# Unused words in the pools, so that tiles read by one-pass matmuls start on multiples of 128 bytes

## The chip, the cores and the metric

The kernel runs on one core of one Trainium2 chip. The metric is the device time of that core in microseconds (us), the median of several runs. The profile comes from one profiled execution; its engines are PE (TensorE matmuls), PEld (TensorE weight loads), DVE (VectorE), ACT (ScalarE), POOL (GpSimd) and SP (the engine that issues most DMAs).

## The reference, cut to what matters

Two layers over a stream of 256 context tokens and 2048 latent tokens, 1024 wide, all in float32. Each layer does, on every token:

```
h      = layer_norm(x) * (1 + scale) + shift           # modulated by c or c_ctx
z      = h @ w_in                                      # 1024 x 3040 columns
y      = concat(hgrn2(z), latent_attention(z), gla(z)) * silu gates
x_new  = layer_norm(ALPHA * x + gate * (y @ w_out)) * ln_g + ln_b
```

The recurrences run in both directions; the attention has 4 heads over all tokens with 128-wide compressed keys and a 64-wide rotary part. The result is the latent stream after layer 1.

## The kernel before, in words

Each layer has three stages, one behind the other, each in a context with its own pools. `project` makes the normed tokens and multiplies them with w_in. `mix` runs attention and recurrences side by side. `output` multiplies by w_out and does the post norm.

**One-pass matmuls.** A float32 operand a is split by `split` into a part hi in the format F32R and a rest lo, also in F32R. The product a b is then three matmuls, hi hi + hi lo + lo hi, each of them one pass through the array. A matmul has a stationary operand (128 columns, loaded by a weight load of its own) and a moving one (256 or 512 columns, streamed past). These are the one-pass matmuls of the kernel, with the pools' tiles that they read:

- L417 in `group`, natural order: stationary hh or hl (the split tokens), moving wh or wl (the split weights), 256 columns (224 in the first weight group), 48 in a row for one pair of token tiles.
- L428 in `group`, transposed order: stationary wh or wl, moving hh or hl, 256 columns, 48 in a row.
- L838 and L850 in `query_group`: mh, ml, urh, url against cqh, cql, 256 columns, 6 in a row for one output tile.
- L888 to L892 in `attend`: stationary qh, ql, rh, rl, moving cth, ctl, ks, up to 512 columns, 5 in a row.
- L913, L914 and L917 in `attend`: stationary cnh, cnl, moving ph, pl, 256 columns.
- L1069 to L1071 in `output`: stationary yhl, moving the 16 weight tiles wh[k], wl[k] (name wo), 512 columns, 24 in a row for one output tile. The first 11 weight tiles lie under tag woa, the last five (wl[5], wh[6], wl[6], wh[7], wl[7]) under tag wob.
- L564: two small ones for the forget gates, with zaT and wa2.

In these rows of a profile the moving operand stands first behind the arrow and the stationary one second (`pj<-wh,hh`). Transposes and the recurrences' matmuls (L774, L790, L801, L623) take plain float32 tiles.

**Where tiles lie.** A pool's tiles are laid in memory one behind the other, by tag in the order of first use, each rounded up to a multiple of 32 bytes for each partition. Pools follow each other in the order in which they are made, and `Route` only names which tags share a pool. So the start of a tile follows from the sizes in front of it. The first tile, ident, starts on a multiple of 128 bytes. In front of mh stand 512 + 32 + 32 + 384 + 4 x 64 + 2 x 64 + 1024 + 32 = 2400 bytes, which is 18 x 128 + 96, so mh starts 96 bytes behind a multiple of 128. What follows in cpool is a multiple of 128, so every stage's first pool starts at 96 as well. In `project` two small pools shift what comes behind them: the side work of layer 0 (bmc, mp, bmd, gcol) adds 288 bytes to multiples of 128, the statistics (st, mv, ve, rs) another 288. In layer 1 a tile `pad` of 16384 bytes stands in place of the side work. In `output` the statistics (sto, mvo, veo, rso) add 288.

The offsets of the operands behind a multiple of 128 bytes, before and after the change, worked out in this way:

| tile | before, layer 0 | before, layer 1 | after, both |
|---|---|---|---|
| hh, hl | 96 | 96 | 0 |
| wh, wl in `project` | 32 | 0 | 0 |
| mh, ml, urh, url, cqh, cql, qh, ql, rh, rl, cth, ctl, ks, cnh, cnl, ph, pl | 96 | 96 | 0 |
| wo under woa | 96 | 96 | 0 |
| wo under wob, yhl | 0 | 0 | 0 |
| wa2, zaT | 64 | 64 | 96 |

A slice of such a tile starts a multiple of 512 bytes behind its start, so the offsets hold for every matmul. The order of instructions on each engine comes from a scheduler that works with priorities and modelled times; a tile that takes the memory of earlier tiles waits until their last readers are done.

Of the kernel before, what the change touches and what calls it, by code (L numbers as in the profile page):

```python
# [31 lines left out]
def view(ap, offset, dims, parts=None):  # L32
    """A free-dimension pattern of its own on the tile behind ap."""
    pd = list(ap.ap[0])
    if parts is not None:
        pd[1] = parts
    return bass.AP(ap.tensor, ap.offset + offset, [pd] + [list(d) for d in dims])


class Route:  # L40
    """Tiles by tag, each from the pool that holds the tag: the order of pools is the order in memory."""
# [12 lines left out]
class Trunk:  # L54
# [17 lines left out]

    def split(self, hi, lo, src, hi_eng="act", lo_eng="dve"):
        """src = hi + lo with both parts in the tensor engine's one-pass format."""
        nc = self.nc
        if hi_eng == "act":
            nc.scalar.copy(hi, src)  # L77
        else:
            nc.vector.tensor_copy(hi, src)
        if lo_eng == "pool":  # L80
            nc.gpsimd.tensor_tensor(lo, src, hi, op=ALU.subtract)
        else:
            nc.vector.tensor_tensor(lo, src, hi, op=ALU.subtract)  # L83

    def rsqrt(self, pool, v, n, name):
        """(v + eps already added) ** -0.5 for a [P, n] tile."""
        r = pool.tile([P, n], F32, tag=name, name=name)
        self.nc.gpsimd.tensor_tensor(r, v, self.mhalf[:, :n], op=ALU.pow)
        return r

    def constants(self):
        nc, io, c = self.nc, self.io, self.cpool
        self.ident = c.tile([P, P], F32, name="ident")
        make_identity(nc, self.ident)
        self.mhalf = c.tile([P, 8], F32, name="mhalf")
        nc.vector.memset(self.mhalf, -0.5)
        # the gated heads' query scale, on the rows of the even and of the odd heads
        self.hm = c.tile([P, 2], F32, name="hm")
        for r in range(4):
            for i in range(2):  # L100
                nc.vector.memset(self.hm[32 * r:32 * r + 32, i:i + 1], float(32.0 ** -0.5) if r % 2 == i else 0.0)
        self.mask = c.tile([P, 6, 64], U8, name="mask")
        with self.tc.tile_pool(name="cm", bufs=1) as cm:
            mf = cm.tile([P, 6, 64], F32, name="mf")
            nc.sync.dma_start(out=mf, in_=io["lmask"])
            nc.vector.tensor_copy(self.mask, mf)

# [1 line left out]
    def scratch(self, l):  # L109
        """Layer l's arrays in DRAM, and its modulation columns."""  # L110
        d, c, nt = self.dpool, self.cpool, self.nt
        S = {}
        S["scT"] = c.tile([P, KD, 2], F32, name=f"scT{l}")
        S["shT"] = c.tile([P, KD, 2], F32, name=f"shT{l}")
        S["gate"] = d.tile([2, D], F32, name=f"gate{l}")
        S["F"] = d.tile([P, self.ntiles, 2, 3, SEG], F32, name=f"dF{l}")
        S["K"] = d.tile([P, self.ntiles, 2, 3, SEG], F32, name=f"dK{l}")
        S["Q"] = d.tile([P, self.ntiles, 4 * SEG], F32, name=f"dQ{l}")
        S["nat"] = d.tile([nt, 1536], F32, name=f"dnat{l}")
        S["cqT"] = d.tile([P, 2, nt], F32, name=f"dcq{l}")  # L120
        S["kT"] = d.tile([P, 2, nt], F32, name=f"dkT{l}")
        S["kN"] = d.tile([P, self.ntiles, P], F32, name=f"dkN{l}")
        S["sb"] = d.tile([P, self.ntiles, 2, 3, 64], F32, name=f"dsb{l}")
        S["y"] = d.tile([nt, D], F32, name=f"dy{l}")
        return S
# [10 lines left out]
    def mod_first(self, S, R, ps, first):  # L136
        """Layer 0's shift and scale as columns."""
# [23 lines left out]
    def mod_rest(self, S0, S1, R, bm0):  # L161
        """Layer 0's gate and layer 1's modulation: products along the free dimension, one column block at a time."""
# [30 lines left out]
        bm = R.tile([P, 24], F32, name="bmd")  # L193
# [10 lines left out]
    def lower_bounds(self, S):  # L204
        """Layer 1's forget-gate floor: the running sum of the softmax over layers less its first term."""
# [20 lines left out]
    def gate_weights(self, l, S, R):  # L226
        """The low-rank gate weights stacked [hi; hi; lo], against gates stacked [hi; lo; hi]."""
# [9 lines left out]
    def latent_weights(self, l, S, R, ps):  # L237
        """The low-rank query and key weights joined: M_h = W_uq,h W_uk,h^T; and the rotary and value ones."""
# [28 lines left out]
    def project(self, l, S, after):  # L267
        """after: the next layer's arrays, where its modulation is worked out beside this projection."""
        nc, io = self.nc, self.io
        with ExitStack() as ctx:  # L270
            R = Route(lambda: self.pool(ctx), "hh hl", "stg gcat gq gkv",
                      "zaT ltn lkd zn zh ltt lqn jk ss rsk rsq ropt ropa ropb gxs gab",
                      "srow wmt jkm mp mc bmc bmd gcol pad", "wraw", "xt st mv ve rs hf", "wh wl")
# [3 lines left out]
            # the first two weight groups run side by side while the first block's tokens come in  # L277
            units = [(b, gs) for b in range(len(blocks))
                     for gs in ([(0, 1)] if b == 0 else [(0,), (1,)]) + [(g,) for g in range(2, self.NGROUP)]]
            h, hf, w, side = {}, {}, {}, iter(())  # L280
            if l == 0:
                bm = self.mod_first(S, R, ps, lambda: hf.update({0: self.normed_pair(l, S, R, ps, 0, plain=True)}))
                side = self.mod_rest(S, after, R, bm)
                for g in range(2):
                    w[0, g] = self.group_weights(l, R, g, first=True)
                self.modulate(S, hf[0], 0)
            else:
                pad = R.tile([P, 64 * 64], F32, name="pad")
                nc.gpsimd.memset(pad[:, 0:1], 0.0)
# [47 lines left out]
    # weight groups in the order in which they run: first column, number of columns  # L337
# [17 lines left out]
    def normed_pair(self, l, S, R, ps, pr, plain=False):  # L355
        """The modulated norm of two token tiles, transposed: [d, k, 256]; plain leaves out the modulation."""
# [47 lines left out]
    def group(self, l, S, R, ps, g, w, h, pairs):  # L404
        """One weight group against a block's token pairs; yields after each pair."""
# [4 lines left out]
        def natural(pr):  # L410
            """[P, tile of the pair, 256]: tokens on partitions, n weight columns."""
# [9 lines left out]
        def transposed(pr):  # L421
            """[P, 128-column block, 256]: weight columns on partitions, the pair's tokens."""
# [12 lines left out]
        def by_tile(o):  # L435
            """[P, block, tile, 128] on a stage that holds tile by tile."""
# [58 lines left out]
    def rope(self, pool, out, src, t, per_tile):  # L495
        """Rotary positions by rows and columns. src [P, n, 64]; out [P, n, 2, 64] holds the result twice.
        n counts tiles from t on (per_tile), or heads of tile t."""
# [23 lines left out]
    def rms(self, pool, pj, n, tag):  # L521
        """[P, 2] reciprocal RMS over n columns of each tile of the pair."""
# [8 lines left out]
    def key_latents(self, S, pp, ps, pj, pr, xs):  # L531
        """RMS norm and rotary positions of a pair's key latents, and their transposes; the forget gates' inputs."""
# [52 lines left out]
    def gla_decay(self, S, pp, xs, pairs):  # L585
        """The forget gates exp(log_sigmoid(x) / 16), both directions of a block."""
# [14 lines left out]
    def head_rows(self, h):  # L601
        """(key slice in a [.., 3*128] natural tile, output rows, output column block, value block)"""
# [6 lines left out]
    def chunk_products(self, rp, rps, kT, vt, name):  # L609
        """Chunk by chunk [P, block, 64]: sum over the chunk's tokens of key x value for all heads."""  # L610
# [7 lines left out]
        # neighbours differ in the array's rows and columns  # L618
# [9 lines left out]
    def back_states(self, S, rp, rps):  # L628
        """States of the backward scans at each chunk's right end, into S["sb"]."""
# [3 lines left out]
        for t in list(range(NCT))[::-1] + list(range(NCT, self.ntiles))[::-1]:  # L633
# [16 lines left out]
            # st[:, c]: the state at chunk c's right end  # L650
# [10 lines left out]
    def recur(self, l, S, rp, rps):  # L661
        """Both scans' outputs, normed and gated, for all token tiles in ascending order."""
# [5 lines left out]
        for t in range(self.ntiles):  # L668
# [9 lines left out]
            if need:  # L678
# [4 lines left out]
                # slots 0 and 1 by token; slots 2 and 3 side by side, chunk by chunk  # L683
# [15 lines left out]
            for lv in range(-1, 6):  # L699
# [20 lines left out]
                if need:  # L720
                    # d = 0: suffix products of the backward decays; d = 1: prefix products of the forward ones
# [36 lines left out]
    def level_scores(self, rps, km, q, c, lv, acc):  # L758
        """acc[(e, j), chunk, slot, i]: key-query products of the pairs that meet at this level."""
# [59 lines left out]
    def query_group(self, S, ap, aps, t):  # L819
        """Query operands of two token tiles: [rank, head, 256] and the rotary [.., head, 128] parts."""  # L820
# [124 lines left out]
    def mix(self, l, S):  # L945
        """Attention and recurrence side by side, into S["y"]."""
        nc = self.nc
        with ExitStack() as ctx:
# [43 lines left out]
            # a tile of the second sweep is worth PACE tiles of the first, and context queries have few keys  # L992
# [17 lines left out]
    def output(self, l, S):  # L1010
        nc, io = self.nc, self.io
        last = l == DEPTH - 1
        with ExitStack() as ctx:
            R = Route(lambda: self.pool(ctx), "yt", "woa", "sto mvo veo rso", "gate", "lng lnb", "z", "xto", "wob", "yhl")
            ps = Route(lambda: self.pool(ctx, psum=True), "low", "pz", "tr")
            nc.vector.memset(ps.tile([P, 512], F32, name="low")[:, 0:1], 0.0)
            gates = {}
# [37 lines left out]
            for t in tiles:  # L1055
# [26 lines left out]
                # the very last rows leave in two parts, the second one worked out meanwhile  # L1082
# [31 lines left out]
def host_arrays(i):  # L1114
    """The inputs laid out for the chip, and tables that depend on shapes alone."""
# [78 lines left out]
```

## Time and profile before

| | us |
|---|---|
| median of 3 runs | 3839.76 |
| lowest and highest run | 3833.27, 3840.97 |
| the profiled execution, first to last instruction | 3840.8 |
| TensorE busy with matmuls in it | 3740.7 |
| VectorE busy | 2529.3 |
| ScalarE busy | 1452.2 |
| GpSimd busy | 187.3 |

The profiled execution's own time is its span; it lies 1.0 us over the median of the runs. Matmuls overlap each other in the profile, so the length shown for one is more than the time from its start to the next one's start. The second is called the spacing here: in a stretch where TensorE has no idle time, it is what one matmul costs.

### The profile page before, as it was taken

The page shows a single profiled execution, that of the slowest core. Times are in us where ns is not written, and L with a number is a line of the kernel's source. Part 1 is how long each engine was busy: PE and PEld are TensorE (multiplying, and loading weights), DVE is VectorE, ACT ScalarE, POOL GpSimd, SP SyncE. Part 2 cuts the span into 40 slices and gives each one's busy share as a digit, 9 for nine tenths or more (in the row PEclk, how much of TensorE's full clock was granted, in tenths as well). Part 3 has the DMA queues.
Part 4 walks back from the last instruction along what each step waited for, and adds up shares of the span by engine and source line. Part 5 has one row for each costly group of instructions (what it writes and reads, how often), then busy time and mean ns, then how long its engine had stood idle before and what let it go on. Part 6 is the DMA issues. An engine that isn't in the chain of part 4 may idle for free.

```text
span 3840.8 us, 82784 instructions
## 1 busy us (share of the span) xinstructions
PE 3740.7 (97%) x34152; PEld 3341.4 (87%) x34152; DVE 2529.3 (66%) x6956; ACT 1452.2 (38%) x2347; POOL 187.3 (5%) x194
## 2 busy tenths in 40 slices
PE   8899999999999999998999999999999999999899
PEld 5899999888888888887879999998888888888777
DVE  6763242577888888776765432426778888888566
ACT  3524242344444444442115252523444444444400
POOL 1000000000000000010110000000000000000111
PEclk9999999999999999999999999999999999999999
DMA  7775453323222212114435453523231212211232
GB/s 253 229 206 155 122 155 108 110 85 92 76 68 62 69 57 69 54 59 167 150 105 181 141 156 101 170 90 118 78 96 49 79 55 69 73 55 33 89 140 104
DMA packets 305850, 415.30 MB, mean 108 GB/s; under 512 B 43008, under 2 KB 235840, under 8 KB 304448
## 3 DMA queue, kind: packets, MB, share of 16 engines
q1 hardware_dynamic: 304032, 407.64, 33.8%
q8 instruction: 269, 4.41, 0.5%
q10 hardware_dynamic: 1440, 2.36, 0.2%
q14 instruction: 109, 0.89, 0.1%
HBM read 290.89 MB, written 119.03 MB: 107 GB/s over the span
## 4 chain that ended last, share of the span: by engine, by line
PE 71%; DVE 2%; DMA 2%; ACT 1%; issue 0%; POOL 0%; SPq 0%; DVEq 0%; ACTq 0%; POOLq 0%
PE pj L417 10%; PE pa L774 7%; PE ptp L924 6%; PE pj L428 5%; PE oc L917 4%; PE oc L913 4%; PE pzo L1069 3%; PE pzo L1070 3%; PE pzo L1071 3%; PE pss L888 3%; PE oc L914 3%; PE pss L889 3%; PE pss L891 3%; PE pss L890 3%; PE pss L892 3%; PE po L801 1%
## 5 line engine op out<-in xcount | busy, mean ns | idle before, releaser
L417 PE MATMUL pj<-wh,hl 128*128 128x256 f32 (+1 forms) x2224 | 623.0, 281 | 8.4 <-DVE hl L83 8.4
L417 PE MATMUL pj<-wh,hh 128*128 128x256 f32 (+1 forms) x2224 | 624.5, 281 | 2.0 <-DVE ve L369 1.2
L417 PE MATMUL pj<-wl,hh 128*128 128x256 f32 (+1 forms) x2224 | 623.1, 280 | 0.0
L77 ACT CAST ph<-ptp 128x512 fp32r<-128x512 f32 x580 | 333.2, 586 | 369.9 <-PE ptp L924 349.6
L83 DVE TENSOR_TENSOR pl<-ptp,ph 128x512 fp32r<-128x512 f32 x580 | 392.9, 686 | 111.2 <-ACT ph L77 109.9
L893 DVE TENSOR_SCALAR_CACHE_REDUCE sx<-pss 128x512 f32<-128x512 f32 (+1 forms) x648 | 399.2, 631 | 79.5 <-PE pss L892 74.2
L417 PEld LDWEIGHTS pj<-wh,hl 128*128 128x128 f32 x2224 | 421.5, 190 | 9.3 <-DVE hl L83 9.3
L417 PEld LDWEIGHTS pj<-wh,hh 128*128 128x128 f32 x2224 | 423.1, 190 | 2.7 <-DVE ve L369 1.6
L417 PEld LDWEIGHTS pj<-wl,hh 128*128 128x128 f32 x2224 | 422.3, 190 | 0.0
L924 PE MATMUL ptp<-ident,sx 128*128 128x128 f32 x2320 | 368.5, 275 | 17.2 <-ACT sx L903 17.2
L903 ACT ACTIVATE sx<-sx,nm 128x2304 f32<-128x2304 f32 (+1 forms) x136 | 288.4, 2121 | 173.5 <-DVE nm L899 171.4
L913 PE MATMUL oc<-ph,cnh 128*128 128x256 f32 x1160 | 346.0, 320 | 5.1 <-ACT ph L77 4.4
L83 DVE TENSOR_TENSOR wl<-wraw,wh 128x1024 fp32r<-128x1024 f32 (+1 forms) x144 | 169.6, 1211 | 238.8 <-ACT wh L77 238.7
L428 PE MATMUL pj<-hh,wh 128*128 128x256 f32 x1136 | 321.0, 283 | 0.0
L428 PE MATMUL pj<-hh,wl 128*128 128x256 f32 x1136 | 319.3, 281 | 0.0
L428 PE MATMUL pj<-hl,wh 128*128 128x256 f32 x1136 | 318.2, 280 | 0.0
L914 PE MATMUL oc<-ph,cnl 128*128 128x256 f32 x1160 | 301.9, 282 | 0.0
L924 PEld LDWEIGHTS ptp<-ident,sx 128*128 128x128 f32 x2320 | 272.8, 141 | 28.0 <-ACT sx L903 19.4
L774 PE MATMUL pa<-qa,km 64*64 64x64 f32 (+1 forms) x4896 | 279.3, 248 | 3.4 <-DVE qa L739 3.1
L888 PE MATMUL pss<-cth,qh 128*128 128x512 f32 (+1 forms) x648 | 269.4, 416 | 5.4 <-DVE sx L893 5.0
L917 PE MATMUL oc<-pl,cnh 128*128 128x256 f32 x1160 | 251.1, 297 | 7.0 <-DVE pl L83 6.8
L774 PEld LDWEIGHTS pa<-qa,km 64*64 64x64 f32 x4896 | 202.4, 134 | 58.4 <-issue 34.3
(241 smaller groups left out, 8035.7 us busy)
## 6 DMA issues: line engine op xcount, KB each, us to landing
wraw<-in_w_in_dram SPq DMA_DIRECT2D x132, 512.0 KB, 4.7
dnat<-stg SPq DMA_DIRECT2D x104, 256.0 KB, 2.1
vg<-dnat SPq DMA_DIRECT2D x34, 512.0 KB, 4.2
yt<-dy SPq DMA_DIRECT2D x34, 512.0 KB, 3.6
wmt<-in_w_modT_dram SPq DMA_DIRECT2D x64, 256.0 KB, 4.0
fa<-dF SPq DMA_DIRECT2D x36, 384.0 KB, 3.3
ka<-dK SPq DMA_DIRECT2D x36, 384.0 KB, 3.3
dK<-stg SPq DMA_DIRECT2D x36, 256.0 KB, 4.1
```

Of the source, the lines that this page charges most:

```text
L77: nc.scalar.copy(hi, src)
L83: nc.vector.tensor_tensor(lo, src, hi, op=ALU.subtract)
L417: nc.tensor.matmul(pj[:, j, :n], h[pr][a][:, k, tk], w[b][:, k, :n], start=(k == 0 and a + b == 0), stop=(k == KD - 1 and a == 1))
L428: nc.tensor.matmul(pj[:, j, :], w[b][:, k, cs], h[pr][a][:, k, :], start=(k == 0 and a + b == 0), stop=(k == KD - 1 and b == 1))
L774: nc.tensor.matmul(pa[rows, po:po + n], km[rows, sl, tk:tk + 64], mv, start=True, stop=True, tile_position=(64 * e, 64 * e))
L888: nc.tensor.matmul(pss[:, :n], G["qh"][hp][:, i, tk], K["cth"][:, ks], start=True, stop=False)
L893: nc.vector.tensor_scalar(sx[:, ks], pss[:, :n], SCALE, None, op0=ALU.mult, op1=ALU.max, accum_out=mx[:, nb:nb + 1])
L903: nc.scalar.activation(sx[:, :nk], sx[:, :nk], AF.Exp, bias=nm, accum_out=sm)
L913: nc.tensor.matmul(oc, K["cnh"][:, ks], ph[:, c, :], start=(kc + c == 0), stop=False)
L914: nc.tensor.matmul(oc, K["cnl"][:, ks], ph[:, c, :], start=False, stop=False)
L917: nc.tensor.matmul(oc, K["cnh"][:, ks], pl[:, c, :], start=False, stop=(kc + c == nch - 1))
L924: nc.tensor.transpose(pt[:, c, i, :], pexp[i][:, (kc + c) * P:(kc + c + 1) * P], self.ident)
```

## The change

A helper `fill` allocates a tile of n words for each partition and clears its first word on GpSimd. It is called for `edge` (8 words) in cpool behind mask, for `edge6` (24 words) in the statistics' pool of `project` in both layers, for `edge4` (16 words) in the side work's pool of layer 0, and for `edgeo` (24 words) in the statistics' pool of `output`. The pad of layer 1 grows from 4096 to 4224 words. The tile bmd takes the memory of bmc (tag bmc) and no longer has its own. No matmul, copy or transfer of the work is added or taken away. The other lines of the diff remove comments and docstrings and keep the line numbers up to the helper; they are left out here.

```diff
+    def fill(self, pool, name, n):
+        self.nc.gpsimd.memset(pool.tile([P, n], F32, name=name)[:, 0:1], 0.0)
...
         self.mask = c.tile([P, 6, 64], U8, name="mask")
+        self.fill(c, "edge", 8)
...
-        bm = R.tile([P, 24], F32, name="bmd")
+        bm = R.tile([P, 24], F32, tag="bmc", name="bmd")
...
-                      "srow wmt jkm mp mc bmc bmd gcol pad", "wraw", "xt st mv ve rs hf", "wh wl")
+                      "srow wmt jkm mp mc bmc bmd gcol pad edge4", "wraw", "xt st mv ve rs hf edge6", "wh wl")
...
+            self.fill(R, "edge6", 24)
             if l == 0:
                 bm = self.mod_first(S, R, ps, lambda: hf.update({0: self.normed_pair(l, S, R, ps, 0, plain=True)}))
                 side = self.mod_rest(S, after, R, bm)
+                self.fill(R, "edge4", 16)
...
-                pad = R.tile([P, 64 * 64], F32, name="pad")
-                nc.gpsimd.memset(pad[:, 0:1], 0.0)
+                self.fill(R, "pad", 4224)
...
-            R = Route(lambda: self.pool(ctx), "yt", "woa", "sto mvo veo rso", "gate", "lng lnb", "z", "xto", "wob", "yhl")
+            R = Route(lambda: self.pool(ctx), "yt", "woa", "sto mvo veo rso edgeo", "gate", "lng lnb", "z", "xto", "wob", "yhl")
             ps = Route(lambda: self.pool(ctx, psum=True), "low", "pz", "tr")
             nc.vector.memset(ps.tile([P, 512], F32, name="low")[:, 0:1], 0.0)
+            self.fill(R, "edgeo", 24)
```

## Rows read from the trace of the kernel before

**Rows 1.** The page: busy time, share of the span and instructions of each engine.
```profile
PE 3740.7 (97%) x34152; PEld 3341.4 (87%) x34152; DVE 2529.3 (66%) x6956; ACT 1452.2 (38%) x2347; POOL 187.3 (5%) x194
```
**Rows 2.** The page: the chain that ended last, shares of the span by engine.
```profile
PE 71%; DVE 2%; DMA 2%; ACT 1%; issue 0%; POOL 0%; SPq 0%; DVEq 0%; ACTq 0%; POOLq 0%
```
**Rows 3.** Windows by stage: stretch and width; busy of each engine; granted clock, DMA share.
```profile
180.00:700.00 520.00, 520.00 (x4517) 519.73 (x4516) 206.00 (x418) 179.53 (x299) 15.17 (x23) 1.00 0.48 145
700.00:1740.00 1040.00, 1021.25 (x10950) 871.80 (x10949) 840.27 (x2686) 455.84 (x725) 38.39 (x37) 1.00 0.24 73
...
1790.00:1990.00 200.00, 200.00 (x938) 163.80 (x938) 141.93 (x224) 25.87 (x49) 27.83 (x23) 1.00 0.39 140
...
2030.00:2610.00 580.00, 580.00 (x4915) 580.00 (x4913) 225.77 (x435) 220.21 (x356) 17.08 (x24) 1.00 0.44 138
```
**Rows 4.** Groups of PE instructions by line: shapes, count, busy us, mean ns of one.
```profile
L417 PE MATMUL pj<-wh,hh 128*128 128x256 f32 (+1 forms) x2224 | 624.5, 281 | 2.0 <-DVE ve L369 1.2 <-DVE hh L79 0.9
...
L913 PE MATMUL oc<-ph,cnh 128*128 128x256 f32 x1160 | 346.0, 320 | 5.1 <-ACT ph L77 4.4 <-ACT os L933 0.3
L428 PE MATMUL pj<-hh,wh 128*128 128x256 f32 x1136 | 321.0, 283 | 0.0
...
L1069 PE MATMUL pzo<-wo,yhl 128*128 128x512 f32 x544 | 219.8, 404 | 9.8 <-DVE z L1072 9.8
```
**Rows 5.** Windows of L417 alone: PE busy and count, PEld, granted clock, DMA.
```profile
230.00:280.00 50.00, 50.00 (x444) 50.00 (x443) 1.00 0.79 194
...
640.00:665.00 25.00, 25.00 (x214) 25.00 (x213) 1.00 0.23 74
2110.00:2135.00 25.00, 25.00 (x216) 25.00 (x215) 1.00 0.42 136
2145.00:2183.00 38.00, 38.00 (x322) 38.00 (x322) 1.00 0.47 153
```
**Rows 6.** Windows of L428 alone, the same columns.
```profile
545.00:592.00 47.00, 47.00 (x401) 47.00 (x400) 1.00 0.66 208
...
2447.00:2502.00 55.00, 55.00 (x461) 55.00 (x460) 1.00 0.64 204
```
**Rows 7.** Timeline of PE in the output stage: start, length, engine, line, operation.
```profile
1815.62 0.40 PE L1069 MATMUL pzo<-wo,yhl 128*128 128x512 f32 x1
...
1819.82 0.40 PE L1069 MATMUL pzo<-wo,yhl 128*128 128x512 f32 x1
...
1820.29 0.39 PE L1071 MATMUL pzo<-wo,yhl 128*128 128x512 f32 x1
...
1821.20 0.38 PE L1049 MATMUL pty<-ident,yt 128*128 128x128 f32 x2
...
1826.26 0.40 PE L1069 MATMUL pzo<-wo,yhl 128*128 128x512 f32 x1
...
1827.65 0.40 PE L1069 MATMUL pzo<-wo,yhl 128*128 128x512 f32 x1
```
**Rows 8.** Timeline of PE: twelve L838 matmuls in a row, first and last, twice.
```profile
785.90 0.28 PE L838 MATMUL pq<-cqh,mh 128*128 128x256 f32 x1
...
787.20 0.28 PE L838 MATMUL pq<-cqh,ml 128*128 128x256 f32 x1
...
1459.19 0.29 PE L838 MATMUL pq<-cqh,mh 128*128 128x256 f32 x1
...
1460.51 0.29 PE L838 MATMUL pq<-cqh,ml 128*128 128x256 f32 x1
```
**Rows 9.** Timeline of PE: four score matmuls in a row, first and last.
```profile
1399.73 0.39 PE L889 MATMUL pss<-ctl,qh 128*128 128x512 f32 x1
...
1400.42 0.39 PE L892 MATMUL pss<-ks,rl 128*128 128x512 f32 x1
```
**Rows 10.** Timeline of POOL: a wo split before the output stage; the pad's clearing.
```profile
1703.19 2.40 POOL L81 TENSOR_TENSOR wo<-woraw,wo 128x1024 fp32r<-128x1024 f32 x1 [12.21 <-ACT wo L77]
...
1992.53 0.10 POOL L289 MEMSET pad<- 128x1 f32 x1 [7.07 <-PE pzo L1071]
```

## The prediction

> **What bounds the kernel now.** I read the page first, from the top: matmuls keep TensorE busy for 3740.7 us of 3840.8, VectorE is at 66%, ScalarE at 38% [rows 1]. The chain that ended last is TensorE for 71% of the span, with nothing else over 2% [rows 2]. Then the windows by stage: in the projections TensorE is busy for 520 us of 520 and 580 of 580, with VectorE at 206 and 226 and the DMA engines below half; in layer 0's output stage it is busy for 200 of 200, VectorE for 142; in layer 0's mix stage for 1021 of 1040, VectorE for 840 [rows 3]. So in projection and output a matmul that costs less shortens the kernel by as much, and there is room before another engine is next. The granted clock is 1.00 in all of these, the 2.4 GHz level, and stays so in what follows.
>
> The change touches nothing of the work. All that it can alter is what a one-pass matmul costs through where its operands lie, so I looked for the spacing of matmuls at each pair of offsets in the table above. The groups by line show lengths, 281 and 283 ns for the 256-column ones [rows 4]; these overlap and tell little. Windows of one line in a stretch without idle time do better: the count includes what began just ahead of the window, so spacing is (width + 0.28 us) / count. In pairs (offset of moving operand, offset of stationary operand), in ns:
>
> (32, 96), L417 in layer 0: 50.28 / 444 = 113.2 in the middle of the stage, but 25.28 / 214 = 118.1 near its end, with the same offsets [rows 5]. (0, 96), L417 in layer 1: 117.0 and 118.9 [rows 5]. (96, 32), L428 in layer 0: 47.28 / 401 = 117.9; (96, 0), L428 in layer 1: 55.28 / 461 = 119.9 [rows 6]. The code of the two layers is the same here; the offset of wh and wl differs.
>
> With 512 columns the output stage holds both pairs in one loop. Of the 24 matmuls of an output tile the first 18 read weights at 96, except one; the last six read weights at 0; yhl is at 0 throughout. From 1815.62 to 1819.82 that is 18 matmuls at 233.3 each; the last six take 1.38 us, 230.0 each, and the last four of them, from 1820.29 to 1821.20, 227.5 [rows 7]. In the next tile the last six take 1.39 us, 231.7 each [rows 7]. So (96, 0) costs 233.3, and (0, 0) settles at 227.5 in one tile and 231.7 in the other.
>
> (96, 96), all of attention: twelve L838 matmuls have eleven spacings in 1.30 us and in 1.32 us, 118.2 and 120.0 [rows 8]; three spacings of score matmuls of 512 columns take 0.69 us, 230.0 [rows 9].
>
> **The change, part by part.** After it every pair but that of L564 is (0, 0). That pair is in the trace only with 512 columns. Its price with 256 columns is bounded below by 113.2, the least that any pair shows, and above by 120.0, the most that a pair of equal offsets shows [rows 5, 8]. I take the nearest row, the same pair of offsets at twice the columns: the mean of 227.5 and 231.7 is 229.6, and half of it 114.8 [rows 7]. Halving is an estimate; (96, 0) supports it, with 233.3 at 512 and 119.9 at 256, half being 116.7, so halves come out a little low [rows 6, 7].
>
> Layer 0, L417: 9 pairs x 8 groups x 48 = 3456 matmuls, 432 of them with 224 columns, which I leave as they are. The 3024 others cost 114.2 now, if four in five are at 113.2 and one at 118.1 (an estimate from the two windows): 3024 x (114.8 - 114.2) = +1.8 us. Layer 0, L428: 9 x 4 x 48 = 1728 x (114.8 - 117.9) = -5.4 us. Layer 1 leaves out context pairs in some groups, so 2784 L417 matmuls of 256 columns, at 118.3 between its two windows: 2784 x -3.5 = -9.7 us. Layer 1, L428: 1680 x (114.8 - 119.9) = -8.6 us. Output: 3 x 544 = 1632 matmuls [rows 4], 17 of 24 at woa, so 1156 x (229.6 - 233.3) = -4.3 us.
>
> Attention goes from one pair of equal offsets to another, and (0, 0) and (96, 96) lie together at 512 columns: 230.0 to 231.7 against 230.0 [rows 7, 9]. I take zero. If the offset itself counts, the 3 x 1160 L913 to L917 and the 612 of L838 and L850 gain up to 119.1 - 113.2 = 5.9 ns each, 24 us, and some 2590 score matmuls 2.5 ns each, 6 us.
>
> The fills: six more clearings on GpSimd of 0.10 us each, the length of the pad's [rows 10], on an engine that is busy for 187 us. A clearing can wait for the earlier readers of its memory. The one of `edgeo` lies on the last recurrence tile's memory, and behind it on GpSimd queue the wo splits, the first of them after 12.21 us of idle time [rows 10]; that idle time hides it. Without it each us of delay would move the splits, and the first pzo matmuls wait for those. The pad's clearing already waits for pzo matmuls at 1992.53 and has the same place as before. bmd now waits for the last reader of bmc, a quarter of the way through the side work, while bmd is used at its end. All of this at zero; above, a few us.
>
> The sum is 1.8 - 5.4 - 9.7 - 8.6 - 4.3 = -26.2 us: 3814.6 on the profiled execution's 3840.8, which is 1.0 over the median of the runs, so 3813.6, rounded to 3813.
>
> The Trainium skill, TensorE: Matmul & The Clock Gate, Part 2: What happens when you issue a matmul, says the opposite of a gain: TensorE reads the moving operand and the next weights through two independent ports, and loading weights takes nothing from the running matmul. By this where the two lie against each other would not matter and the sum would be zero. The trace disagrees as far as it goes: four pairs, four spacings, in code that is otherwise the same [rows 5, 6].
>
> **The rivals.** *Only the distance between the two operands counts* (the other side). Then (0, 0) costs at 256 columns what (96, 96) does, 118.2 to 120.0 [rows 8]. For it: the two lie together at 512 columns. Against it: those L838 rows are short runs between other work. The place is L417 of layer 0, which loses its 113.2. At the middle, 119.1: 3024 x 4.9 + 1728 x 1.2 + 2784 x 0.8 - 1680 x 0.8 = +17.8, less 4.3 in the output stage, +13.5 us: 3853. At 118.2 it is 3845, at 120.0 3861. The 9216 matmuls make 9.2 us for each ns, so the sum turns at 117.6; measurably slower (0.2%, 7.7 us, about what a measurement of this kernel can tell from no change) begins at 118.5, measurably faster at 116.8.
>
> *Fully settled everywhere.* Every aligned matmul costs 113.2 or 227.5, in attention too. The projections give 3.0 + 8.1 + 14.2 + 11.3, the output stage 6.7, attention 30: 73 us, 3766. Against it: two tiles of the same stage settle differently [rows 7].
>
> *Offsets are not the cause.* Layer 0 moves from 113.2 to 118.1 without any offset changing [rows 5], so a break in the stream can do what I credit to memory. Then little changes: 3840. Against it: layer 1 shows 113.2 in none of its windows. The skill's rule above is this rival's ground.
>
> **How the numbers follow.** The forecast 0.47, with 3797 to 3828 as its own range (aligned spacing 113.2 to 116.5); settled everywhere 0.12; distance 0.28; not the cause 0.13. Faster by over 0.2%: the first two but for 0.02, 0.57. Within 0.2%: that 0.02, the last case's 0.13, and 0.04 for the part of distance below 118.5, 0.19. Slower: the rest of distance, 0.24. The range, 3776 to 3856, reaches two thirds of the way into the settled case and past the middle of the distance case.
>
> **What would show it.** In the profile after: L417 and L428 windows of both layers at one spacing, near 114.8; the first 18 matmuls of an output tile as cheap as the last six; attention's spacings as before; the stages' ends earlier by some 4 us in projection 0, 18 in projection 1, 2 in each output. Wrong would be 118 or more at L417 in layer 0, a layer that is slower than before, or a first pzo matmul that is late because GpSimd stood at a clearing.

## The result, and the profile after

The changed kernel takes 3874.06 us (median of 4 runs, 3871.70 to 3875.16), the kernel before 3838.93 beside it: ratio 1.0090, 95% interval 1.0076 to 1.0104. It is slower by 35 us, on the other side of the forecast and 18 us above the range. Its profiled execution spans 3873.1 us.

The page of the changed kernel, busy time by engine:

```profile
PE 3773.4 (97%) x34152; PEld 3369.1 (87%) x34152; DVE 2530.6 (65%) x6956; ACT 1449.9 (37%) x2346; POOL 186.2 (5%) x200
```

Against [rows 1] TensorE is busy for 32.7 us more with the same 34152 matmul records, and the span grew by 32.3. So the time did not go into waiting. Windows of L423 alone (L417 of before; the helper moves all later lines by six), two in layer 0 and two in layer 1, and behind them two of L434 (L428 of before); the columns are those of [rows 5]:

```profile
230.00:280.00 50.00, 50.00 (x419) 50.00 (x418) 1.00 0.72 171
655.00:680.00 25.00, 25.00 (x211) 25.00 (x210) 1.00 0.23 74
2133.00:2158.00 25.00, 25.00 (x210) 25.00 (x210) 1.00 0.40 128
2170.00:2208.00 38.00, 38.00 (x319) 38.00 (x319) 1.00 0.42 130
```

```profile
550.00:597.00 47.00, 47.00 (x394) 47.00 (x393) 1.00 0.68 212
2472.00:2527.00 55.00, 55.00 (x460) 55.00 (x460) 1.00 0.64 201
```

The same stretch of layer 0 that began 444 matmuls in 50 us [rows 5] now begins 419: 50.28 / 419 = 120.0 ns instead of 113.2. The other three windows give 119.8, 120.4 and 120.0, those of L434 120.0 and 120.2. So the forecast of one spacing for both lines and both layers came true, at 120.0 and not at 114.8. It is not a matter of the windows chosen: over all spacings of the trace between 256-column matmuls of one of these lines, breaks left out, the means are 119.9 to 120.0 in each layer (before: L417 114.4 and 118.2, L428 117.7 and 120.0). Attention went from one pair of equal offsets to another and stayed where it was, as its largest group shows beside [rows 4], 321 ns long against 320:

```profile
L919 PE MATMUL oc<-ph,cnh 128*128 128x256 f32 x1160 | 346.8, 321 | 6.2 <-ACT ph L81 5.5 <-ACT os L939 0.3
```

In the output stage, the second and the twentieth of 24 pzo matmuls in a row, 18 spacings apart in the timeline of PE:

```profile
1832.50 0.39 PE L1077 MATMUL pzo<-wo,yhl 128*128 128x512 f32 x1
...
1836.68 0.40 PE L1077 MATMUL pzo<-wo,yhl 128*128 128x512 f32 x1
```

That is 4.18 / 18 = 232.2 ns, 1.1 less than the 233.3 of [rows 7]; the last matmuls of a tile, which had their offsets at 0 before, do not get cheaper (231.3 on the mean of the trace, 230.6 before).

From the spacings the loss in the projections is 3024 x 5.5 + 1728 x 2.3 + 2784 x 1.7 = 16.6 + 4.0 + 4.7 = 25 us (L434 in layer 1 stays at 120.0), and next to nothing in the output stage. Some 10 us are left for something else.

### The profile page after: what moved, and what is told of

It is laid out like the page before. It is cut to its first block, busy times and chain, and to the rows that moved or that the text cites. A ratio compares the mean times of both kernels' runs of the same rounds, so it can differ in the third digit from the quotient of the medians.

```text
span 3873.1 us, 82783 instructions
## 1 busy us (share of the span) xinstructions
PE 3773.4 (97%) x34152; PEld 3369.1 (87%) x34152; DVE 2530.6 (65%) x6956; ACT 1449.9 (37%) x2346; POOL 186.2 (5%) x200
## 5 line engine op out<-in xcount | busy, mean ns | idle before, releaser
L423 PE MATMUL pj<-wh,hl 128*128 128x256 f32 (+1 forms) x2224 | 630.2, 284 | 8.1 <-DVE hl L87 8.0
L423 PE MATMUL pj<-wh,hh 128*128 128x256 f32 (+1 forms) x2224 | 632.0, 284 | 1.9 <-DVE hh L83 1.9
L423 PE MATMUL pj<-wl,hh 128*128 128x256 f32 (+1 forms) x2224 | 630.2, 283 | 0.0
L423 PEld LDWEIGHTS pj<-wh,hl 128*128 128x128 f32 x2224 | 427.6, 193 | 9.2 <-DVE hl L87 9.2
L423 PEld LDWEIGHTS pj<-wh,hh 128*128 128x128 f32 x2224 | 428.7, 193 | 2.5 <-DVE hh L83 2.5
L423 PEld LDWEIGHTS pj<-wl,hh 128*128 128x128 f32 x2224 | 428.6, 193 | 0.0
L434 PE MATMUL pj<-hh,wh 128*128 128x256 f32 x1136 | 323.4, 285 | 0.0
L434 PE MATMUL pj<-hh,wl 128*128 128x256 f32 x1136 | 322.3, 284 | 0.0
L434 PE MATMUL pj<-hl,wh 128*128 128x256 f32 x1136 | 322.0, 283 | 0.0
```

The costliest lines, as they stand in the source:

```text
L423: nc.tensor.matmul(pj[:, j, :n], h[pr][a][:, k, tk], w[b][:, k, :n], start=(k == 0 and a + b == 0), stop=(k == KD - 1 and a == 1))
L434: nc.tensor.matmul(pj[:, j, :], w[b][:, k, cs], h[pr][a][:, k, :], start=(k == 0 and a + b == 0), stop=(k == KD - 1 and b == 1))
```

## The experiments

Two questions: which property of the offsets sets the spacing, and what the other 10 us are. The theory after the result: the distance between the two operands counts (moving less stationary, modulo 128), and 0 is dear at 256 columns. Rivals: the start of one operand counts by itself; the fills or the new place of bmd cost time whatever the offsets.

**fill_only.** All edits of the change stay, but the fills are sized so that every offset is what it was before.

```diff
-        self.fill(c, "edge", 8)
+        self.fill(c, "edge", 32)
-            self.fill(R, "edge6", 24)
+            self.fill(R, "edge6", 16)
-                self.fill(R, "edge4", 16)
+                self.fill(R, "edge4", 8)
-                self.fill(R, "pad", 4224)
+                self.fill(R, "pad", 4080)
-            self.fill(R, "edgeo", 24)
+            self.fill(R, "edgeo", 32)
```

> The kernel after with other fill sizes, so that every one-pass operand has its offset of before again (hh, hl 96; wh, wl 32 in layer 0 and 0 in layer 1; attention 96), while every fill, the tag of bmd and the order of TensorE's instructions stay those of after. Theory 1 (the offsets, through the distance between moving and stationary operand, set the spacing): both projections return to the spacings of before, 113 to 118 ns for L417 of layer 0 instead of 120, so 25 us of the 35 are gone; what remains, about 10 us in the two mix stages, belongs to the order: 3846 to 3852 us. Rival (the fills and the new order cost it all): 3874 us as after.

3856.17 us, ratio 1.0039 (1.0025 to 1.0053) to the kernel before beside it, 4 us above what was expected. Windows of L423, one in each layer, and the page's busy times:

```profile
249.00:289.00 40.00, 40.00 (x357) 40.00 (x356) 1.00 0.74 175
...
2154.00:2192.00 38.00, 38.00 (x323) 38.00 (x323) 1.00 0.43 131
```

```profile
PE 3752.2 (97%) x34152; PEld 3345.7 (87%) x34152; DVE 2533.1 (66%) x6956; ACT 1450.6 (38%) x2346; POOL 186.2 (5%) x200
```

The spacings are back, 40.28 / 357 = 112.8 and 38.28 / 323 = 118.5. So the offsets cause the 120.0. But 16 us remain that have nothing to do with offsets, and most of them are busy time too: 3752.2 against 3740.7 [rows 1].

**all32.** The changed kernel with an edge of 16 words instead of 8, so that every operand starts at 32 and every distance is still 0.

```diff
-        self.fill(c, "edge", 8)
+        self.fill(c, "edge", 16)
```

> The kernel after with 8 more words in edge, so that every tile moves 32 bytes on: all one-pass operands at 32, distance 0 as in after. Theory 1 (distance): nothing changes, L417 and L428 at 120 ns, 3874 us. Rival (the moving operand's own offset counts, and 32 was the good place for wh and wl in layer 0): L417 falls to 113 to 115 ns in both layers, about 32 us less, 3842 us.

3872.99 us, ratio 1.0085 (1.0070 to 1.0100), the time of the changed kernel. A window of L423 in layer 0 and one of L434 in layer 1:

```profile
230.00:280.00 50.00, 50.00 (x419) 50.00 (x418) 1.00 0.79 192
...
2475.00:2530.00 55.00, 55.00 (x461) 55.00 (x460) 1.00 0.64 201
```

50.28 / 419 = 120.0 and 55.28 / 461 = 119.9: a multiple of 128 is not special, equal offsets cost the same at 32.

**w64.** The changed kernel with wh and wl at 64 and hh, hl at 0.

```diff
-            self.fill(R, "edge6", 24)
+            self.fill(R, "edge6", 40)
```

> The kernel after with 16 more words in edge6, so that wh and wl lie 64 bytes behind a multiple of 128 and hh, hl at 0. Theory 1 (distance between the operands, modulo 128): 64 is the distance that layer 0 had before, so L417 at 113.3 to 117.8 ns in both layers and L428 near 117.7, against 120 now: 5808 x 5.5 + 3408 x 2.2 ns = 39 us less than after, 3835 us. Rival (each operand's own offset counts, and 32 for the weights or 96 for the tokens was the good place): no return to 113, 3874 us or more.

3849.38 us, ratio 1.0023 (1.0014 to 1.0032), 14 us more than expected. Windows of L423 in layer 0 and of L434, twice in layer 0:

```profile
230.00:280.00 50.00, 50.00 (x427) 50.00 (x426) 1.00 0.79 189
```

```profile
150.00:174.00 24.00, 24.00 (x214) 24.00 (x213) 1.00 0.83 278
...
542.00:589.00 47.00, 47.00 (x401) 47.00 (x400) 1.00 0.71 220
```

L423, moving 64 and stationary 0, sits at 50.28 / 427 = 117.8 throughout. L434, moving 0 and stationary 64, shows two levels with one pair of offsets, 24.28 / 214 = 113.5 and 47.28 / 401 = 117.9. At a distance of 64 it therefore matters which of the two has the lower offset, and the distance alone is not the whole rule. It is 25 us better than the changed kernel all the same; the expected 39 had L423 5.5 ns cheaper than 120.0, and it is 2.2.

**before_w32.** The kernel before with a pad of 8 words more, so that layer 1 has layer 0's offsets: wh and wl at 32, 64 bytes from hh and hl.

```diff
-                pad = R.tile([P, 64 * 64], F32, name="pad")
+                pad = R.tile([P, 64 * 64 + 8], F32, name="pad")
```

> The kernel before with 8 more words in the pad of layer 1, so that wh and wl of layer 1 lie at 32 as in layer 0, with hh, hl at 96 as ever. Both theories about offsets: layer 1 takes the spacings of layer 0, L417 from 118.2 to 114.4 ns and L428 from 120.0 to 117.7: 2784 x 3.8 + 1680 x 2.3 ns = 14 us less than before, 3825 us. Rival (the layers differ by something else than the offsets): 3839 us as before.

3823.37 us, ratio 0.9953 (0.9939 to 0.9968): faster than both kernels. Two windows of L417 and one of L428, all in layer 1:

```profile
2103.00:2128.00 25.00, 25.00 (x223) 25.00 (x223) 1.00 0.44 140
2138.00:2176.00 38.00, 38.00 (x338) 38.00 (x337) 1.00 0.46 148
```

```profile
2431.00:2486.00 55.00, 55.00 (x469) 55.00 (x469) 1.00 0.64 203
```

L417 shows 113.4 and 113.3, L428 117.9, as layer 0 always had [rows 5, 6].

**own_bmd and tag_only.** Both ask for the 16 us of fill_only. Compared place by place in the traces, 6053 of TensorE's 34152 matmul records stand elsewhere in the changed kernel than in the kernel before, from the 123rd on; without the sharing of bmd's memory only 6 do, besides 14 neighbours that start within 1 ns of each other. So own_bmd keeps all offsets at 0 and gives bmd its memory back; tag_only adds to the kernel before nothing but the sharing, in a slot made as much larger as bmd's is missed.

```diff
 own_bmd, on the changed kernel
-        bm = R.tile([P, 24], F32, tag="bmc", name="bmd")
+        bm = R.tile([P, 24], F32, name="bmd")
-            self.fill(R, "edge6", 24)
+            self.fill(R, "edge6", 16 if l == 0 else 24)
-                self.fill(R, "edge4", 16)
 tag_only, on the kernel before
-        bm = R.tile([P, 24], F32, name="bmc")
+        bm = R.tile([P, 48], F32, tag="bmc", name="bmc")[:, 0:24]
-        bm = R.tile([P, 24], F32, name="bmd")
+        bm = R.tile([P, 48], F32, tag="bmc", name="bmd")[:, 0:24]
```

> The changed kernel, but bmd has memory of its own again; the fill of the side work is dropped and the one of the statistics in layer 0 is 16 words, so that every one-pass matmul still has both operands on a multiple of 128. TensorE then does its work in the order of the kernel before, but for 6 places. Theory (the shared memory of bmd and bmc changes the order of instructions, and that costs some 15 us; the rest of the loss is the distance 0): 3858 us, 3853 to 3863. Rival (the clearings of the fills, or the mere places of other tiles, cost it): 3874, as the changed kernel. All L423 and L434 matmuls of 256 columns at 120.0 ns in either case.

> The kernel before with one edit: bmd takes the memory of bmc, which is made 96 bytes larger, so that no operand of a one-pass matmul changes its offset and nothing is filled. Theory (the order costs some 15 us): 3855 us, 3849 to 3860, spacings of L417 and L428 as before. Rival (the sharing is harmless, the fills cost it): 3840.

own_bmd: 3859.52 us, ratio 1.0051 (1.0036 to 1.0066), 14.5 us less than the changed kernel. tag_only: 3849.39, ratio 1.0026 (1.0017 to 1.0036), 10.6 us more than the 3838.75 of the kernel before beside it. In own_bmd L422 keeps its 120.0, 50.28 / 419:

```profile
230.00:280.00 50.00, 50.00 (x419) 50.00 (x418) 1.00 0.68 167
```

The mix stage shows the price. In each of four kernels, from the first to the last of layer 0's 1168 ptp transposes (one line's instructions in a short stretch; the last two figures are the first and last start): own_bmd, then the kernel with the pad alone, both in the order of before:

```profile
L929 PE MATMUL ptp<-ident,sx x2: 273/302/330, 734.5 to 734.7; 128*128 128x128 f32 x2
...
L929 PE MATMUL ptp<-ident,sx x4: 273/273/274, 1781.3 to 1781.7; 128*128 128x128 f32 x4
```

```profile
L924 PE MATMUL ptp<-ident,sx x2: 272/300/329, 715.1 to 715.3; 128*128 128x128 f32 x2
...
L924 PE MATMUL ptp<-ident,sx x4: 272/272/273, 1763.3 to 1763.6; 128*128 128x128 f32 x4
```

and tag_only and the changed kernel, both in the new order:

```profile
L924 PE MATMUL ptp<-ident,sx x2: 273/302/331, 714.7 to 714.9; 128*128 128x128 f32 x2
...
L924 PE MATMUL ptp<-ident,sx x4: 272/273/273, 1768.4 to 1768.7; 128*128 128x128 f32 x4
```

```profile
L930 PE MATMUL ptp<-ident,sx x2: 273/302/330, 733.5 to 733.6; 128*128 128x128 f32 x2
...
L930 PE MATMUL ptp<-ident,sx x4: 273/273/273, 1787.0 to 1787.3; 128*128 128x128 f32 x4
```

1781.7 - 734.5 = 1047.2 and 1048.5 us against 1054.0 and 1053.8, whatever the offsets. Layer 1's mix stage tells the same, 1011.3 and 1008.8 against 1012.4 and 1015.5.

The traces also show where. Nearly all the displaced records lie in the later part of the two mix stages. From the 12873rd matmul record to the 16703rd (layer 0, 1402 to 1773 us in the kernel before), five kernels in the old order (before, before_w32, own_bmd, and ph64 and w0h64 further down) take 370.8 to 373.6 us and the five in the new one (tag_only, fill_only, w64, all32 and the changed kernel) 377.3 to 379.8. From the 26148th to the 28779th (layer 1) it is 230.2 to 230.5 against 233.5 to 233.7. That makes 10 us. From the 9874th to the 12279th, where the order is the same, all ten take 208.1 to 208.5; and from the 29910th on displaced records cost nothing, 347.3 to 349.2 us in either order.

So the sharing costs 10 to 16 us through the order of the instructions, some 10 of it in these two stretches, and the fills cost nothing that shows: own_bmd has all but one of them, and lies 20.8 us over the kernel before, where the spacings alone give 25.

**m256 and m512.** One-pass matmuls alone, 48 in a row for each pair of offsets; the reference's work is left out. The last 16 pairs follow each other without a break.

```python
for j in range(2):
    for k in range(8):
        for a, b in ((0, 0), (0, 1), (1, 0)):
            nc.tensor.matmul(pj[:, j, :], H[:, a, 4 * s + 256 * k + 128 * j:4 * s + 256 * k + 128 * j + 128],
                             W[:, b, 4 * m + 256 * k:4 * m + 256 * k + 256],
                             start=(k == 0 and a + b == 0), stop=(k == 7 and a == 1))
```

> Only one-pass matmuls of 256 columns, 48 in a row for each pair of offsets, moving operand at 0, 16, .. 112 bytes and stationary one at 0, 16, .. 112 bytes behind a multiple of 128: 64 pairs, eight transposes ahead of each; it leaves out all of the reference's work. Theory (only the distance modulo 128 counts): the 64 spacings fall into 8 values by distance, the same wherever the two lie; distance 0 at 120.0 ns, 64 at 113.3 or 117.8, 32 and 96 between 117 and 120. Rival (the place of one operand itself counts): pairs of one distance differ by several ns.

> The same with 512 columns. Theory: again by distance alone; 0 at about 230 ns, 96 (moving minus stationary) at about 233, as in the output stage; for 64 no trace shows a price, an estimate from twice the 256-column one less the 10 ns by which 512 columns stay under twice 120 is 217 to 226. Rival: all within 1 ns of each other, so that nothing is to be had in attention's score matmuls and in the output stage.

The timeline of PE at the end of m256. The second letter of a name gives the moving operand, the third the stationary one (a, c, e, g: 0, 32, 64, 96); a row is 48 matmuls, so the next row's start less its own, over 48, is the spacing:

```profile
428.10 5.90 PE L51 MATMUL paa<-mov,sta 128*128 128x256 f32 x48
433.84 5.82 PE L51 MATMUL pca<-mov,sta 128*128 128x256 f32 x48
439.50 5.82 PE L51 MATMUL pea<-mov,sta 128*128 128x256 f32 x48
445.15 5.91 PE L51 MATMUL pga<-mov,sta 128*128 128x256 f32 x48
...
473.64 5.61 PE L51 MATMUL pae<-mov,sta 128*128 128x256 f32 x48
479.09 5.84 PE L51 MATMUL pce<-mov,sta 128*128 128x256 f32 x48
484.76 5.92 PE L51 MATMUL pee<-mov,sta 128*128 128x256 f32 x48
490.52 5.82 PE L51 MATMUL pge<-mov,sta 128*128 128x256 f32 x48
```

Equal offsets: paa 5.74 / 48 = 119.6, pee 120.0. Moving 64, stationary 0 (pea): 117.7; the other way round (pae): 113.5. The same pairs in m512:

```profile
775.35 11.09 PE L51 MATMUL paa<-mov,sta 128*128 128x512 f32 x48
786.28 11.37 PE L51 MATMUL pca<-mov,sta 128*128 128x512 f32 x48
797.48 11.16 PE L51 MATMUL pea<-mov,sta 128*128 128x512 f32 x48
808.48 11.38 PE L51 MATMUL pga<-mov,sta 128*128 128x512 f32 x48
...
863.97 11.36 PE L51 MATMUL pae<-mov,sta 128*128 128x512 f32 x48
875.17 11.36 PE L51 MATMUL pce<-mov,sta 128*128 128x512 f32 x48
886.37 11.07 PE L51 MATMUL pee<-mov,sta 128*128 128x512 f32 x48
897.27 11.37 PE L51 MATMUL pge<-mov,sta 128*128 128x512 f32 x48
```

Here equal offsets are the cheapest of the rows shown, paa 10.93 / 48 = 227.7 and pee 227.1; pae takes 233.3, pea 229.2, pca 233.3. So the price that was expected for 64 apart with 512 columns, 217 to 226, was too low. Equal offsets are among the dearest of these rows with 256 columns and the cheapest with 512. The strict form of the theory fell: in the first 64 rows, at starts of 16 bytes more than a multiple of 32, equal offsets settle at 116.7 to 118.3 at 256 columns, and the pairs of one distance spread over several ns: with the stationary operand 48 bytes further on, from 116.7 at (48, 96) to 123.6 at (0, 48), the dearest of all 64 pairs.

**ph64 and ph64o.** Can attention gain too? ph64 is before_w32 with ph and pl 64 bytes from cnh and cnl; ph64o adds a fill to the output stage that brings all its operands to 96.

```diff
+                o = 16 - self.flip
+                self.flip = o
-                ph = ap.tile([P, 2, 256], F32R, tag="ph", bufs=2, name="ph")
+                ph = ap.tile([P, 528], F32R, tag="ph", bufs=2, name="ph")[:, o:o + 512].rearrange("p (c n) -> p c n", c=2)
...
 ph64o also
+            nc.gpsimd.memset(R.tile([P, 24], F32, name="edgeo")[:, 0:1], 0.0)
```

> The kernel before with wh and wl of layer 1 at 32 (pad of 4104 words), and ph and pl 64 bytes from cnh and cnl: ph and pl are tiles of 528 words, of which by turns the last and the first 512 are used, so that the moving operand of L915, L916 and L919 (L913, L914 and L917 of before, two lines on) starts at 32 and the stationary one at 96. No order of instructions changes. Theory (at 256 columns a distance of 64 costs 113.3 or 117.8 where equal offsets cost 118 to 120): of 3480 matmuls, six in a row, five spacings of six gain 0.7 to 5.2 ns, 2 to 15 us; from the 3823 of the kernel with the pad alone to 3815, 3808 to 3821. Rival (six in a row are too few to settle, and nothing is gained): 3823.

> The same, and a fill of 24 words in the statistics' pool of the output stage, by which wob and yhl go from 0 to 96 and all output matmuls of 512 columns have both operands at 96. Theory (at 512 columns equal offsets are the cheapest, 226.7 ns when settled against 233.3 at 96 apart, some 231 in runs of 24): 1156 matmuls gain about 2 ns, so 2 us less than the kernel without the fill, 3813; alone that can hardly be told from nothing in the time, but the spacing of the first 18 matmuls of an output tile is to fall from 233 to 231 or less. Rival (the start of yhl or of the weights counts, not their distance): the spacing stays at 233.

(The three lines kept their numbers L913, L914 and L917.) ph64: 3823.19 us, ratio 0.9956 (0.9942 to 0.9969); ph64o: 3819.62, ratio 0.9949 (0.9937 to 0.9962). Neither can be told from before_w32 by its time. The groups of the first and second of the six matmuls, ph64 and then before_w32:

```profile
L913 PE MATMUL oc<-ph,cnh 128*128 128x256 f32 x1160 | 344.4, 319 | 6.3 <-ACT ph L77 5.6 <-ACT os L935 0.3
L914 PE MATMUL oc<-ph,cnl 128*128 128x256 f32 x1160 | 299.7, 281 | 0.0
```

```profile
L913 PE MATMUL oc<-ph,cnh 128*128 128x256 f32 x1160 | 346.2, 320 | 6.5 <-ACT ph L77 5.9 <-ACT os L933 0.3
L914 PE MATMUL oc<-ph,cnl 128*128 128x256 f32 x1160 | 302.1, 282 | 0.0
```

They are busy for 4.2 us less, no more, and the spacing of neighbours among the six is 118.6 ns on the mean of the trace (ph64) against 119.4: six in a row between transposes do not come down to 113. In ph64o the first 16 spacings of an output tile are 232.6 on the mean against 233.1 in ph64: not 231 or less, and not unchanged, so neither theory nor rival held.

**w0h64.** The pad of before_w32, and all of the pools 96 bytes further: hh and hl at 64, wh and wl at 0.

```diff
+        nc.gpsimd.memset(c.tile([P, 24], F32, name="edge")[:, 0:1], 0.0)
```

> The kernel before with the pad of layer 1 at 4104 words and 24 unused words more in front of mh, so that in both layers wh and wl start at 0 and hh and hl at 64: L418 (L417 of before) has moving 0, stationary 64, L429 has moving 64, stationary 0; attention goes from 96, 96 to 64, 64. The distances are those of the kernel with the pad alone, 3823 us, where the pairs are (32, 96) and (96, 32), L417 at 114.5 ns and L428 at 117.7. Theory A (at 256 columns the distance alone sets the spacing): the same, 3823, L418 at 114.5 and L429 at 117.7. Theory B (the pair 0, 64 holds the lower level of 113.3 throughout, as it did where such matmuls ran by themselves, while 32, 96 loses it at breaks): 5808 x 1.1 = 6 us less, 3817, L418 at 113.3 to 113.6. Theory C (the pair with the moving operand ahead takes either level by chance): L418 anywhere from 113.3 to 117.8, up to 20 us more, 3823 to 3843.

3822.35 us, ratio 0.9958 (0.9944 to 0.9972), the same. Windows of L418, early and late in layer 0:

```profile
230.00:280.00 50.00, 50.00 (x444) 50.00 (x443) 1.00 0.74 179
640.00:665.00 25.00, 25.00 (x214) 25.00 (x214) 1.00 0.24 75
```

113.2 and then 118.1, the very counts of [rows 5] at (32, 96). The mean of L418 is 114.3, that of L429 117.7. The pair (0, 64) behaves as (32, 96) and does not hold the lower level either. That is theory A; both levels occur where the moving operand has the lower offset. In the kernel before a row of L417 keeps one level from break to break: 532 matmuls from 220.3 us on lie at 113.3, 286 from 635.6 us on at 117.8.

## Why the prediction was wrong

*The failed step: the price of (0, 0) at 256 columns.* The prediction halved a 512-column spacing, 229.6, and took 114.8. The runs give 120.0, the upper bound of that step. Halving carries a price of one width to another where the pairs do not even keep their order: in m512 equal offsets are the cheapest (227.1 to 227.7 against 229.2 and 233.3), in m256 they are among the dearest (119.6 to 120.0, where 64 apart gives 113.5 and 117.7). The 229.6 itself was near what the output stage shows for (0, 0), 230.6 on the mean before and 231.3 to 232.2 after. The check on the halving, (96, 0) at 233.3 and 119.9, was a single pair of another distance, dear at both widths, and could not show this. The sum of the four projection terms was -21.9 and came out as +25.

*The rows that were right.* The twelve L838 rows at equal offsets [rows 8] had the answer, 118.2 to 120.0 with 256 columns. The prediction set them behind a row of twice the width because they are short runs. The nearest row was the one of the same width and the same distance: among equal offsets 0, 32, 64 and 96 cost the same with 256 columns, as all32 and m256 show.

*The rival of the distance* was right about equal offsets and about its place, L417 of layer 0, though not in saying that only the distance counts (w64, m256). Its price was at its upper end: with 120.0 it gave 3861, and own_bmd, the change without the new order, measured 3859.5. That the two lie so close is in part luck: the 3861 holds a gain of 4.3 us in the output stage, which came to 0.7. The chance of 0.28 for it, against 0.47 and 0.12 for two cases that own_bmd and all32 exclude, was too small: the prediction itself had found (0, 0) and (96, 96) at one price with 512 columns.

*The step that was taken at zero: bmd in bmc's place.* "above, a few us" was meant for a wait. No wait of that size came; the place of more than a sixth of TensorE's matmul records changed, and that costs 10 to 16 us (tag_only, fill_only, and own_bmd against the changed kernel). This lifts the time from 3860, already above the range's 3856, to 3874. Some 10 us of it lie in the two stretches of displaced records named above. Which of the displaced instructions costs it, and why, stays open: the loss is for the most part busy time, and no group of waits grew by as much.

*Right:* the fills, at zero; attention, unchanged; one spacing for both lines and layers. The output stage's gain of 4.3 us was too high: over all 1632 matmuls the mean spacing of the trace, breaks left out, went from 232.4 to 232.0 ns, which is 0.7 us.

*The rule of independent ports* in the Trainium skill, TensorE: Matmul & The Clock Gate, Part 2: What happens when you issue a matmul, which the prediction cites, read as a rule for the time of a matmul, would make such an edit cost nothing. The runs do not bear that out: 113.2 against 120.0 ns for each matmul, at the full granted clock of 1.00, with the same matmuls in the same order but for 6 of them (own_bmd).

## What to carry to other kernels

Where matmuls of 256 columns follow each other in long rows and bound the time, try the stationary and the moving tile 64 bytes apart modulo 128, with the moving tile at the lower offset (0 or 32); aligning both to 128 bytes is as dear as any pair of multiples of 32 measured here, and 32 bytes more of padding than before gave 0.5%. A tile can be moving in one line and stationary in another, as hh and wh are here, so that only one of the two gets the good side: before_w32 gives it to the line with more matmuls, w64 to the other. Take the price of an operation from a row of its own size, and never scale one size to another for a resource whose rule is unknown. An edit that "only" shares a tile's memory gives the scheduler another dependency, and here it gave another order: compare the queues of both programs before calling it free.

## What the runs showed of the hardware

The spacing of one-pass matmuls, each with a weight load of its own, depends on where both operands lie modulo 128 bytes, at a granted clock of 1.00. At 256 columns: 119.6 to 120.0 ns at equal offsets that are multiples of 32, and at (96, 0) as well; 117.7 at 64 apart with the stationary operand at the lower offset; 113.2 or 118 at 64 apart with the moving one at the lower offset, where the level changes at a break and then stays, up to 60 us in the row of 532. At 512 columns: 227.1 to 227.7 at equal offsets in an unbroken stream, 231 to 232 in runs of 24, and 229.2 to 233.3 in the other rows shown. Why the two widths differ, and what chooses between the two levels, no run here tells.

Nor does any run show at 256 columns that the pattern repeats after 128 bytes and not only after 256: by the layout of the programs, each pair of offsets of the projections and of m256 has the same distance modulo 256 wherever it occurs. In the changed kernel's output stage yhl lies 128 bytes (modulo 256) from the weights under woa and 0 from those under wob, and the spacings there are 232.2 and 231.3 ns, which settles nothing.
